# Low part of every fourth weight chunk: from a VectorE subtraction to an accumulating DMA

## The chip, the core and the metric

The kernel runs on one core of a Trainium2 chip. The metric is the device time of one execution in microseconds (us). In two timed executions the kernel before took 1624.39 and 1624.61 us, median 1624.5 us. A difference of 2% of this, about 32 us, is about what a measurement of this kernel can tell from no change.

## The reference

One encoder block over 256 tokens of width 2048 in float32. All of its large products are with weight matrices:

```python
xn = rms_norm(h, norm1_g[l])
proj = xn @ w_in[l]
z_a, q, c_kv, q_idx, k_idx, w_idx, gates = jnp.split(proj, cuts, axis=-1)
y_a = spatial_gating_unit(jax.nn.gelu(z_a), ...)
y_b = indexer_sparse_attention(q, rms_norm(c_kv, ...), q_idx, k_idx, w_idx, w_uk[l], w_uv[l])
g_a, g_b = jnp.split(jax.nn.sigmoid(gates), 2, axis=-1)
mixed = g_a * (y_a @ w_oa[l]) + g_b * (y_b @ w_ob[l])
h = h + mixed @ w_out[l]
hn = rms_norm(h, norm2_g[l])
h = h + (jax.nn.silu(hn @ w_ff_gate[l]) * (hn @ w_ff_up[l])) @ w_ff_down[l]
```

The projections, the attention's key and value matrices, the output matrices and the feed-forward network together hold some 300 MB of weights. Each weight is read once.

## The kernel before

Every product against a weight matrix is done as three passes of TensorE. An operand is split exactly into h, its upper 12 mantissa bits in the type float32r, and l, the rest; h\*h, l\*h and h\*l are added up in PSUM. The split of a weight is made on the chip, chunk by chunk, in `wchunk` (L73 to L82). A chunk is 128 partitions by 1024 float32, 512 KB, and holds two k tiles of 512 columns. Its way has four steps:

1. SP's queue issues the load of `raw` from DRAM (L80).
2. ScalarE copies `raw` to `wh` with rounding to float32r (L67): the part h.
3. VectorE subtracts, `wl = raw - wh` (L68): the part l.
4. TensorE multiplies with `wh` and `wl`.

The tiles `raw`, `wh` and `wl` come from a pool with four buffers each. So the split of chunk i+4 may be written when TensorE has done its last product with chunk i, and the load of chunk i+4 may start when VectorE has subtracted chunk i. Chunks are made in the order in which TensorE uses them, and each engine runs its instructions in the order in which they are written to its queue.

Two helpers use the chunks. `nat_group` (L89) makes blocks of 512 columns for both tiles of 128 tokens: the weights are the moving operand, 12 products of 512 columns per chunk, 6 for each of the two k tiles. For each it calls `mm3` (L84), whose second product (L86) is the first to read `wl`. `tr_group` (L104) makes transposed blocks for the index queries, the queries and the keys: the weights are the stationary operand, 24 products of 256 columns per chunk, and the third of them (L120) is the first to read `wl`.

The program goes through: the latent and the index keys (16 chunks of 592 columns), index queries and top keys, branch A's values (`v`), attention four heads at a time beside branch A's gates (`q`, `k`, `vv`, `u`), position mixing, gates and branch outputs (`g`, `oa`, `ob`), the output projection (`out`), and the feed-forward network in blocks of 512 columns (`fg` gate, `fu` up, `fd` down). A full group is 8 chunks. After a group its two PSUM banks are taken out, by ScalarE for `v`, `u`, `g` and `fg` (Gelu, Sigmoid or Silu), by VectorE for the others. There are 544 chunks of 1024 columns that go through the pool of four; 8 more, the last ones of `w_ff_down`, are split into tiles that are kept to the end.

The program is written with a scheduler that sets each engine's order from priorities and semaphores; the kernel does not write an order by hand.

Of the kernel before, what the change touches and what calls it, by code (L numbers as in the profile page):

```python
# [32 lines left out]
MARK = -3.0e38  # L33
WARM = 8  # matmuls of zeros that open the clock gate


@with_exitstack
def block_kernel(ctx: ExitStack, tc: tile.TileContext, a, out):
    """Every product against a weight matrix is float32 = three float32r passes: an operand is
    split exactly into h (its upper 12 mantissa bits, rounded) and l (the rest, 12 bits), and  # L40
    h*h + l*h + h*l is accumulated in float32."""
    nc = tc.nc
# [20 lines left out]
    def split(h, l, src, scale=None):  # L63
        """h + l = src (times a scale per partition), exactly."""
        hf = h.bitcast(F32)
        if scale is None:
            nc.scalar.activation(h, src, AF.Copy)  # L67
            nc.vector.tensor_tensor(l, src, hf, op=ALU.subtract)  # L68
        else:
            nc.scalar.activation(h, src, AF.Copy, scale=scale)  # L70
            nc.vector.scalar_tensor_tensor(l, src, scale, hf, op0=ALU.mult, op1=ALU.subtract)

    def wchunk(src, cols, keep=False):  # L73
        raw = wp.tile([P, 1024], F32, tag="raw", name="raw")
        if keep:
            h, l = (t_tile(z).rearrange("p a b -> p (a b)") for z in ("kept_h", "kept_l"))
        else:
            h = wp.tile([P, 1024], F32R, tag="wh", name="wh")
            l = wp.tile([P, 1024], F32R, tag="wl", name="wl")
        nc.sync.dma_start(raw[:, :cols], src)  # L80
        split(h[:, :cols], l[:, :cols], raw[:, :cols])
        return h, l  # L82
# [6 lines left out]
    def nat_group(w, ks, x, name):  # L89
        """[tokens, 512] blocks of x @ w for both token tiles. w: [chunks, 128, 1024] in DRAM;  # L90
        ks: its k tiles; x(k) -> the k tile's (h, l), [128, 256] each."""
        acc = [acc_tile(f"{name}_{t}") for t in range(2)]
        for c in range(len(ks) // 2):
            wh, wl = wchunk(w[c], 1024)
            for j in range(2):
                i = 2 * c + j
                xh, xl = x(ks[i])
                for t in range(2):
                    s = slice(t * P, (t + 1) * P)
                    mm3(acc[t], xh[:, s], xl[:, s], wh[:, j * 512:(j + 1) * 512],  # L100
                        wl[:, j * 512:(j + 1) * 512], i == 0, i == len(ks) - 1)
        return acc

    def tr_group(w, ks, x, name, bank=acc_tile, beside=None):  # L104
        """(x @ w).T for 512 columns of w: two banks of [128 columns, 2, 256 tokens]. beside(c) is
        called after each chunk."""
        acc = [bank(f"{name}_{b}").rearrange("p (c t) -> p c t", c=2) for b in range(2)]
        for c in range(len(ks) // 2):
            wh, wl = wchunk(w[c], 1024)
            for j in range(2):  # L110
                i = 2 * c + j
                xh, xl = x(ks[i])
                for ct in range(4):
                    s = slice(j * 512 + ct * P, j * 512 + (ct + 1) * P)
                    o = acc[ct // 2][:, ct % 2, :]
                    last = i == len(ks) - 1
                    nc.tensor.matmul(o, wh[:, s], xh, start=(i == 0 and ct % 2 == 0), stop=False,  # L117
                                     skip_group_check=True)
                    nc.tensor.matmul(o, wh[:, s], xl, start=False, stop=False, skip_group_check=True)  # L119
                    nc.tensor.matmul(o, wl[:, s], xh, start=False, stop=last, skip_group_check=True)  # L120
            if beside is not None:
                beside(c)
        return acc

    def rsqrt(dst, src, mul, add, m, name):
        """dst = 1 / sqrt(src * mul + add), [128, m]: Newton's steps from the bits' guess, each left
        with a factor (a power of two) that the last product takes out."""
        v = sp.tile([P, m], F32, tag=f"rs_v{m}", name=f"{name}_v", bufs=2)
# [14 lines left out]
    def transposed(src, name, h, l, scale=None):  # L143
        """src [128 tokens, 2, 512] -> h, l [128, 4, 256 tokens]."""
        for b in range(2):
# [11 lines left out]

# [1 line left out]
    # while the first loads run: the activation table, and the tensor engine's clock  # L159
    warm = const.tile([P, 512], BF16, name="warm")  # L160
# [31 lines left out]
    def sumsq(ss, src, n):  # L192
        """ss[:, n, t] = the sums of squares of src [128, 2, 512]'s rows."""
        for t in range(2):
            junk = sp.tile([P, 512], BF16, tag="junk", name="junk")
            nc.scalar.activation(junk, src[:, t], AF.Square, accum_out=ss[:, n, t:t + 1])
# [9 lines left out]

# [1 line left out]
    KS = list(range(KT))  # L208
# [58 lines left out]

# [1 line left out]
    index_queries(1, acc_tile)  # L269
# [22 lines left out]
    for hp in range(8):  # L292
        score_pair(hp)
    # keep: 0 where a key is kept, else a large negative; [tile 1's 256 keys | tile 0's 128]
    keep = sp.tile([P, T + P], F32, name="keep")
    for t in (1, 0):
        w = (t + 1) * P
        nc.vector.memset(score[t][0:CHUNK, w - CHUNK:w], NEG)
        for i in range(TOPK // 8):
# [4 lines left out]
                                op0=ALU.is_gt, op1=ALU.mult)  # L304
    # r1 * B_HEAD_DIM ** -0.5, for tile 1 and tile 0
    ascale = sp.tile([P, 2], F32, name="ascale")
    for t in range(2):
        nc.vector.tensor_scalar(ascale[:, 1 - t:2 - t], r1[:, t:t + 1], P ** -0.5, None, op0=ALU.mult)

# [1 line left out]
    stats = sp.tile([P, 2, 4, 6], F32, name="stats")  # L311
# [34 lines left out]

# [1 line left out]
    yb = []  # L348
# [53 lines left out]

# [1 line left out]
    ws = n_tile("ws").rearrange("p a b -> p (a b)").rearrange("p (g q) -> p g q", g=GROUPS)  # L404
# [21 lines left out]

# [1 line left out]
    def gate(g):  # L428
# [22 lines left out]

# [1 line left out]
    ss2 = sp.tile([P, 4, 2], F32, name="ss2")  # L453
# [13 lines left out]

# [1 line left out]
    at = []  # L469
# [17 lines left out]

    # the last block's weights stay split on chip, so that token tile 0 is through before tile 1
    ends = (4, 8, NFB - 1)
# [55 lines left out]
def _layout(np, i):  # L545
    """The arrays as the program reads them: only cut, transposed and joined."""
    x = np.asarray(i["x"])[0]
# [8 lines left out]
    z, q, c, qi, ki, wi, g = np.split(w_in, cuts, axis=1)  # L556
    col = lambda v: np.asarray(v).reshape(-1, P).T  # noqa: E731
    ln = np.stack([np.asarray(i["a_ln_g"])[0].reshape(4, 512), np.asarray(i["a_ln_b"])[0].reshape(4, 512)], 1)
# [40 lines left out]
```

## Time and profile before

| | |
|---|---|
| timed executions | 1624.39 and 1624.61 us |
| median | 1624.5 us |
| span of the profiled execution, first to last instruction | 1624.0 us |
| what lies around the span, against the median | 0.5 us |
| bytes moved over the span | 307.54 MB |
| engines with the most busy time | TensorE, then its weight loads, VectorE, ScalarE |

The profile is one execution with hardware records of each instruction. Its span is within 0.5 us of the timed median, so a term worked out from its rows can be set against the median as it stands. In the rows PE is TensorE's products, PEld its weight loads, DVE VectorE, ACT ScalarE, POOL GpSimd, and SPq the queue of SP that issues the loads. A row names the line, the engine, the operation, and the tiles as out<-in.

Ends of matmuls are modelled and matmuls overlap, so a row's 0.39 us is longer than the step from one matmul's start to the next. Steps are read here from the starts.

### The profile page before, as it was taken

How to read it: one execution, taken by the hardware profiler on the slowest of the kernel's cores; microseconds unless marked ns; L12 is line 12 of the kernel's file. 1: busy time of each engine (PE TensorE's matmuls, PEld its weight loads, DVE VectorE, ACT ScalarE, POOL GpSimd, SP SyncE). 2: the span in 40 equal slices, each digit the busy share in tenths (PEclk: the TensorE clock that was granted, in tenths of full speed). 3: DMA queues.
4: the chain of work that ended last, by engine and by line, in shares of the span. 5: the costliest groups of instructions: out<-in, count | busy, mean ns of one | idle time of the engine just before them, and what ended most of it. 6: DMA issues, size and time to landing. Idle time of an engine off the chain costs nothing.

```text
span 1624.0 us, 20315 instructions
## 1 busy us (share of the span) xinstructions
PE 1613.2 (99%) x7954; PEld 1358.6 (84%) x7954; DVE 893.8 (55%) x1084; ACT 742.9 (46%) x891; POOL 1.6 (0%) x8
## 2 busy tenths in 40 slices
PE   9999999999999999999999999999999999999997
PEld 8988989889788888888888888888888888888886
DVE  5695665565754444555556444455545454554575
ACT  6554464554544444444444444444344444334452
POOL 0000000000000000000000000000000000000000
PEclk9999999999999999999999999999999999999999
DMA  8646555555545555555655555555655555555671
GB/s 302 214 138 201 187 168 182 170 177 175 163 161 192 193 193 194 193 183 196 236 186 185 194 185 190 186 191 186 194 191 192 186 191 188 193 192 194 218 253 59
DMA packets 88128, 307.54 MB, mean 189 GB/s; under 512 B 10272, under 2 KB 10528, under 8 KB 88032
## 3 DMA queue, kind: packets, MB, share of 16 engines
q1 hardware_dynamic: 88032, 306.25, 57.2%
q8 instruction: 62, 1.02, 0.2%
q14 instruction: 34, 0.28, 0.0%
HBM read 304.11 MB, written 2.10 MB: 189 GB/s over the span
## 4 chain that ended last, share of the span: by engine, by line
PE 99%; DMA 0%; DVE 0%; ACT 0%; SPq 0%; issue 0%; ACTq 0%
PE fg L85 5%; PE fg L86 5%; PE fg L87 5%; PE fu L86 5%; PE fu L87 5%; PE fu L85 5%; PE fd L87 4%; PE fd L85 4%; PE fd L86 4%; PE g L86 4%; PE g L85 4%; PE g L87 4%; PE q L120 2%; PE q L119 2%; PE q L117 2%; PE u L87 2%
## 5 line engine op out<-in xcount | busy, mean ns | idle before, releaser
L68 DVE TENSOR_TENSOR wl<-raw,wh 128x1024 fp32r<-128x1024 f32 (+1 forms) x560 | 678.9, 1212 | 668.6 <-ACT wh L67 668.2
L67 ACT ACTIVATE wh<-raw 128x1024 fp32r<-128x1024 f32 (+1 forms) x560 | 587.8, 1050 | 764.9 <-PE fu L87 139.4
L86 PE MATMUL fg<-wl,hh 128*128 128x512 f32 x352 | 137.8, 392 | 0.0
L87 PE MATMUL fg<-wh,hl 128*128 128x512 f32 x352 | 137.7, 391 | 0.0
L85 PE MATMUL fg<-wh,hh 128*128 128x512 f32 x352 | 137.1, 390 | 0.0
L85 PE MATMUL fu<-wh,hh 128*128 128x512 f32 x352 | 136.9, 389 | 0.0
L86 PE MATMUL fu<-wl,hh 128*128 128x512 f32 x352 | 136.9, 389 | 0.0
L87 PE MATMUL fu<-wh,hl 128*128 128x512 f32 x352 | 136.9, 389 | 0.0
L86 PE MATMUL fd<-wl,ah 128*128 128x512 f32 x320 | 124.8, 390 | 0.0
L87 PE MATMUL fd<-wh,al 128*128 128x512 f32 x320 | 124.8, 390 | 0.0
L85 PE MATMUL fd<-wh,ah 128*128 128x512 f32 x320 | 124.6, 389 | 0.0
L87 PE MATMUL g<-wh,xl 128*128 128x512 f32 x256 | 100.9, 394 | 0.0
L85 PE MATMUL g<-wh,xh 128*128 128x512 f32 x256 | 100.7, 393 | 0.0
L86 PE MATMUL g<-wl,xh 128*128 128x512 f32 x256 | 99.9, 390 | 0.0
L85 PEld LDWEIGHTS fu<-wh,hh 128*128 128x128 f32 x352 | 66.1, 188 | 13.7
L86 PEld LDWEIGHTS fu<-wl,hh 128*128 128x128 f32 x352 | 66.1, 188 | 13.7
L87 PEld LDWEIGHTS fu<-wh,hl 128*128 128x128 f32 x352 | 66.1, 188 | 13.7
L85 PEld LDWEIGHTS fg<-wh,hh 128*128 128x128 f32 x352 | 66.1, 188 | 13.5
L86 PEld LDWEIGHTS fg<-wl,hh 128*128 128x128 f32 x352 | 66.1, 188 | 13.4
L87 PEld LDWEIGHTS fg<-wh,hl 128*128 128x128 f32 x352 | 66.2, 188 | 13.2
L120 PE MATMUL q<-xh,wl 128*128 128x256 f32 x256 | 72.4, 283 | 0.0
L119 PE MATMUL q<-xl,wh 128*128 128x256 f32 x256 | 72.4, 283 | 0.0
(220 smaller groups left out, 2722.7 us busy)
## 6 DMA issues: line engine op xcount, KB each, us to landing
raw<-in_w_fg SPq DMA_DIRECT2D x88, 512.0 KB, 3.3
raw<-in_w_fu SPq DMA_DIRECT2D x88, 512.0 KB, 3.3
raw<-in_w_fd SPq DMA_DIRECT2D x88, 512.0 KB, 3.3
raw<-in_w_z SPq DMA_DIRECT2D x64, 512.0 KB, 3.3
raw<-in_w_g SPq DMA_DIRECT2D x64, 512.0 KB, 3.3
raw<-in_w_q SPq DMA_DIRECT2D x32, 512.0 KB, 3.3
raw<-in_w_oa SPq DMA_DIRECT2D x32, 512.0 KB, 3.3
raw<-in_w_ob SPq DMA_DIRECT2D x32, 512.0 KB, 3.3
```

The source lines that it names most:

```text
L67: nc.scalar.activation(h, src, AF.Copy)
L68: nc.vector.tensor_tensor(l, src, hf, op=ALU.subtract)
L85: nc.tensor.matmul(o, lh, rh, start=start, stop=False, **kw)
L86: nc.tensor.matmul(o, lh, rl, start=False, stop=False, **kw)
L87: nc.tensor.matmul(o, ll, rh, start=False, stop=stop, **kw)
L117: nc.tensor.matmul(o, wh[:, s], xh, start=(i == 0 and ct % 2 == 0), stop=False, skip_group_check=True)
L119: nc.tensor.matmul(o, wh[:, s], xl, start=False, stop=False, skip_group_check=True)
L120: nc.tensor.matmul(o, wl[:, s], xh, start=False, stop=last, skip_group_check=True)
```

## The change

For every fourth call of `wchunk` the low part is made in another way, if the chunk has 1024 columns and isn't one of the kept ones. ScalarE writes h as before, and then a second time into `wl`, with the factor -1: `wl = -h`. Then GpSimd's queue issues a DMA that reads the chunk from DRAM once more and adds it to what stands in `wl`. VectorE has no part in it.

```diff
+    n_chunks = [0]
+
     def wchunk(src, cols, keep=False):
         raw = wp.tile([P, 1024], F32, tag="raw", name="raw")
...
         nc.sync.dma_start(raw[:, :cols], src)
-        split(h[:, :cols], l[:, :cols], raw[:, :cols])
+        n_chunks[0] += 1
+        if keep or cols < 1024 or n_chunks[0] % 4:
+            split(h[:, :cols], l[:, :cols], raw[:, :cols])
+        else:
+
+            nc.scalar.activation(h, raw, AF.Copy)
+            nc.scalar.activation(l, h.bitcast(F32), AF.Copy, scale=-1.0)
+            nc.gpsimd.dma_start(l, src, accum_op=ALU.add)
         return h, l
```

All other lines of the diff take comments away; lines move by up to 9. L67 and L68 stay, the two new ScalarE lines are L88 and L89, and the new DMA is L90; the products L85, L86 and L87 become L94, L95 and L96.

There are 136 such DMAs. Since a full group has 8 chunks, they fall on the fourth and the eighth chunk of every full group, and their `wl` is always the same one of the four buffers.

On ScalarE's queue, before, around the fourth chunk of an up group `fu`: two Silu's take the gate group's banks out, and then the split of the fourth chunk follows.

```order
559 L67 ACTIVATE wh_8332<-raw_8331 128x1024 [waits DMAHW1_49,DVE_49,PE_49]
560 L67 ACTIVATE wh_8350<-raw_8349 128x1024 [waits DMAHW2_49,DVE_49,PE_49]
561 L475 ACTIVATE s2_8308<-fg2_0_8162,r2_r_7520 128x512 [waits PE_49]
562 L475 ACTIVATE s2_8308<-fg2_1_8163,r2_r_7520 128x512 [waits PE_49]
563 L67 ACTIVATE wh_8368<-raw_8367 128x1024 [waits DMAHW3_49,DVE_49]
564 L67 ACTIVATE wh_8386<-raw_8385 128x1024 [waits DMAHW4_49,DVE_49,PE_49]
565 L67 ACTIVATE wh_8404<-raw_8403 128x1024 [waits DMAHW5_49,DVE_49,PE_49]
```

The same place on ScalarE's queue in the changed kernel, one block later (`fg3` in place of `fg2`):

```order
665 L67 ACTIVATE wh_8731<-raw_8730 128x1024 [waits DMAHW1_49,DVE_49,PE_49]
666 L67 ACTIVATE wh_8749<-raw_8748 128x1024 [waits DMAHW2_49,DVE_49,PE_49]
667 L484 ACTIVATE s3_8707<-fg3_0_8559,r2_r_7592 128x512 [waits PE_49]
668 L484 ACTIVATE s3_8707<-fg3_1_8560,r2_r_7592 128x512 [waits PE_49]
669 L88 ACTIVATE wh_8767<-raw_8766 128x1024 [waits DMAHW3_49,Activation_49]
670 L89 ACTIVATE wl_8768<-wh_8767 128x1024 [waits DMASW5_49,Activation_49]
671 L67 ACTIVATE wh_8786<-raw_8785 128x1024 [waits DMAHW4_49,DVE_49,PE_49]
672 L67 ACTIVATE wh_8804<-raw_8803 128x1024 [waits DMAHW5_49,DVE_49,PE_49]
```

The chunk's `wh` keeps its place behind the two Silu's; the `wl` of L89 stands between it and the next chunk's `wh`. Its wait is for the accumulating DMA before (DMASW5), which wrote the same buffer.

On TensorE's queue, before, the first products with that fourth chunk (`wl_8682` is its low part):

```order
5289 L87 MATMUL fu3_1_8625<-wh_8663,hl1_7147 128x512
5290 L85 MATMUL fu3_0_8624<-wh_8681,hh1_7146 128x512 [waits Activation_49]
5291 L86 MATMUL fu3_0_8624<-wl_8682,hh1_7146 128x512 [waits DVE_49]
5292 L87 MATMUL fu3_0_8624<-wh_8681,hl1_7147 128x512
5293 L85 MATMUL fu3_1_8625<-wh_8681,hh1_7146 128x512
```

The same products in the changed kernel (`wl_8768` is the low part):

```order
5289 L96 MATMUL fu3_1_8711<-wh_8749,hl1_7215 128x512
5290 L94 MATMUL fu3_0_8710<-wh_8767,hh1_7214 128x512 [waits Activation_49]
5291 L95 MATMUL fu3_0_8710<-wl_8768,hh1_7214 128x512 [waits DMASW6_49]
5292 L96 MATMUL fu3_0_8710<-wh_8767,hl1_7215 128x512
5293 L94 MATMUL fu3_1_8711<-wh_8767,hh1_7214 128x512
```

No product has moved here; the chunk's second product waits for the DMA (DMASW6) where it waited for VectorE. On SP's queue the load of the fourth chunk behind such a chunk waits for ScalarE instead of VectorE.

## Rows read from the trace of the kernel before

**Rows 1.** The page: busy us, share of the span, instructions, by engine

```profile
PE 1613.2 (99%) x7954; PEld 1358.6 (84%) x7954; DVE 893.8 (55%) x1084; ACT 742.9 (46%) x891; POOL 1.6 (0%) x8
```

**Rows 2.** The page: the chain that ended last, shares by engine

```profile
PE 99%; DMA 0%; DVE 0%; ACT 0%; SPq 0%; issue 0%; ACTq 0%
```

**Rows 3.** The waits of PE: waiter <- waited for: us, times, longest

```profile
PE warm_ps L166 <- DVE warm L161: 1.2, 1, 1.2
PE kv L85 <- ACT xh L70: 0.6, 1, 0.6
```

**Rows 4.** Groups by shape on ACT, DVE: count | busy us, mean ns | idle

```profile
L67 ACT ACTIVATE wh<-raw 128x1024 fp32r<-128x1024 f32 x544 | 576.6, 1060 | 757.4 <-PE fu L87 139.4 <-PE fg L87 121.6 <-PE fd L87 109.7
...
L68 DVE TENSOR_TENSOR wl<-raw,wh 128x1024 fp32r<-128x1024 f32 x544 | 666.5, 1225 | 659.9 <-ACT wh L67 659.5
```

**Rows 5.** Timeline inside an fu group: start us, us, engine, what [idle before <-releaser]

```profile
1001.19 0.39 PE L87 MATMUL fu<-wh,hl 128*128 128x512 f32 x1
...
1001.42 0.39 PE L85 MATMUL fu<-wh,hh 128*128 128x512 f32 x1
...
1001.62 1.06 ACT L67 ACTIVATE wh<-raw 128x1024 fp32r<-128x1024 f32 x1 [1.66 <-PE fu L87]
1001.64 0.39 PE L86 MATMUL fu<-wl,hh 128*128 128x512 f32 x1
...
1002.71 1.23 DVE L68 TENSOR_TENSOR wl<-raw,wh 128x1024 fp32r<-128x1024 f32 x1 [1.49 <-ACT wh L67]
...
1004.34 1.06 ACT L67 ACTIVATE wh<-raw 128x1024 fp32r<-128x1024 f32 x1 [1.66 <-PE fu L87]
...
1005.43 1.23 DVE L68 TENSOR_TENSOR wl<-raw,wh 128x1024 fp32r<-128x1024 f32 x1 [1.50 <-ACT wh L67]
```

**Rows 6.** Timeline of ACT where an fg group ends

```profile
1038.03 1.06 ACT L67 ACTIVATE wh<-raw 128x1024 fp32r<-128x1024 f32 x1 [1.66 <-PE fg L87]
1040.07 1.37 ACT L475 ACTIVATE s<-fg,r_r 128x512 f32<-128x512 f32 x2 [0.98 <-PE fg L87]
1041.33 1.05 ACT L67 ACTIVATE wh<-raw 128x1024 fp32r<-128x1024 f32 x1
```

**Rows 7.** Timeline of ACT inside a q group (transposed)

```profile
312.74 1.06 ACT L67 ACTIVATE wh<-raw 128x1024 fp32r<-128x1024 f32 x1 [1.77 <-PE q L119]
315.62 1.06 ACT L67 ACTIVATE wh<-raw 128x1024 fp32r<-128x1024 f32 x1 [1.82 <-PE q L119]
```

**Rows 8.** DMA of the page: queue share; issues xcount, KB, median us to landing

```profile
q1 hardware_dynamic: 88032, 306.25, 57.2%
...
raw<-in_w_fu SPq DMA_DIRECT2D x88, 512.0 KB, 3.3
...
xn<-in_x SPq DMA_DIRECT2D x4, 512.0 KB, 8.8
```

**Rows 9.** DMA busy tenths, 1001.58 to 1012.46 us, 40 slices; a load then

```profile
DMA  4199598980009589992000977988410069699840
...
raw<-in_w_fg SPq DMA_DIRECT2D x4, 512.0 KB, 4.3
```

**Rows 10.** Windows: stretch, length, busy PE PEld DVE ACT POOL, PEclk, DMA, GB/s

```profile
0.00:10.00 10.00, 8.16 (x28) 5.62 (x29) 4.34 (x9) 6.07 (x11) 1.63 (x8) 1.00 0.78 254
...
1610.00:1624.00 14.00, 5.20 (x35) 4.61 (x33) 6.98 (x20) 3.80 (x10) 0.00 (x0) 0.75 0.30 111
```

## The prediction

> **What bounds the kernel now.** I began with the busy times and the chain that ended last. PE is busy for 1613.2 of 1624.0 us [rows 1], and the chain is PE for 99% of its length [rows 2]. Then the waits of PE: 1.2 and 0.6 us in all, both in the start [rows 3]. So nothing that VectorE, ScalarE or the DMA queues do holds PE up today, and the subtraction that the change takes away is not waited for. VectorE stands idle for 659.9 us before those subtractions, until ScalarE's `wh`, and ScalarE in turn waits for PE's last product with a chunk [rows 4]. The supply runs at PE's pace and has slack. A gain could come only out of the 1.8 us of waits and the two ends of the program, which have no such chunk. The question is whether the new way of making `wl` still fits into the slack.
>
> The slack is read from the timeline of one group [rows 5]. At 1001.19 PE starts its last product with a chunk; at 1001.42 it goes on to the next. At 1001.62 ScalarE starts `wh` in the buffer that came free, and the next `wh` starts at 1004.34: a chunk takes PE 2.72 us. The product at 1001.64 is the first that reads `wl` in the chunk begun at 1001.42. The chunk now being split is the one three later, so its `wl` is read first at 1001.64 + 3 x 2.72 = 1009.80, or 8.18 us after `wh` starts. Today `wl` is ready at 1002.71 + 1.23 = 1003.94. That leaves 5.9 us unused.
>
> **The change, part by part.** It removes 136 VectorE subtractions of 1.225 us, 167 us, beside waits [rows 4]: worth nothing by itself. It adds 136 copies on ScalarE; by the row for the same shape 1.060 us each, 144 us [rows 4], which lifts ScalarE from 742.9 to 887 us, 55% of the span. Four chunks take ScalarE 5 x 1.06 = 5.3 of 10.88 us, so this is hidden as well. The next chunk's `wh` does not begin until 2.72 us after this one's, and the two copies take 2.12. Where a bank's take-out stands before them, the next `wh` is late by some tenths, within its 5.9 us of slack.
>
> What isn't hidden by anything else is the chain behind the copies. `wh` ends at 1.06, `-h` at 2.12; the hand-over to the next engine costs 0.03 (1002.68 to 1002.71 in [rows 5]). The accumulating DMA can be issued 2.15 us after `wh` starts and must have landed at 8.18. **Its margin is 6.03 us** from issue to landing. Two kinds of chunk have another margin:
>
> - Behind a group that ScalarE takes out. The regular `wh` would start at 1038.03 + 2.72 = 1040.75; it starts at 1041.33, behind two Silu's [rows 6]. Margin 6.03 - 0.58 = 5.45 us. By the order of ScalarE's queue that is the fourth chunk behind 4 `v`, 4 `u`, 8 `g` and 11 `fg` groups: 27 chunks.
> - In transposed groups a chunk takes PE 315.62 - 312.74 = 2.88 us [rows 7], 0.16 longer, three times: margin 6.5 us. These are 8 chunks of queries and 4 of index queries, 12 in all.
>
> The other 97 are taken as ordinary. If a DMA lands later than its margin, PE stands still at the chunk's second product, and everything behind it on PE's queue with it; so do the next `wh`s, which wait for PE. GpSimd's queue has nothing else but the next such DMA, 10.88 us later. A stall cannot be won back: the chain for the next chunk in this buffer begins when PE has left this one. So each microsecond over the margin counts in full, 136 times.
>
> **How long does the DMA take?** No row of this trace shows an accumulating DMA or one issued by GpSimd, so it is bounded from both sides. From below: the plain load of the same 512 KB lands 3.3 us after issue [rows 8]; at that price it is hidden, and the change costs nothing. From above: 8.8 us, the longest median landing of 512 KB in this program, beside the crowded loads of the start [rows 8]. That would be 97 x 2.77 + 27 x 3.35 + 12 x 2.3 = 387 us. Less than nothing is excluded at both ends, because PE doesn't wait today.
>
> Between them I build it up. Loads hold the 16 engines for 57.2% of 1624.0 us [rows 8], 929 us for 306.25 MB, or 1.59 us per 512 KB. Adding needs a second operand: what stands in `wl` must be read as well as the chunk. If reads set the pace, that is another 1.6 us: 3.3 + 1.6 = 4.9 us. And it isn't alone. In four chunk times the engines show four bursts of some 2 us with gaps of about 0.7 us between them [rows 9], and in that stretch a plain load already lands after 4.3 us in place of 3.3. With 3.2 us of data, a transfer that begins to move some 4 us after `wh` starts is still moving when the load for the following chunk comes (that one is issued behind the next subtraction, at 1005.43 + 1.23 = 1006.66, or 5.0 us [rows 5]). Sharing with it costs up to that load's own 1.6 us: 6.5 us. I take the 6.5, the end with a full collision, because the issue by software on GpSimd is not in the sum and can only add to it. It is also close to two plain landings one behind the other, 6.6 us.
>
> With 6.5: 97 ordinary chunks x 0.47 = 46 us, 27 chunks behind a take-out x 1.05 = 28 us, 12 transposed ones x 0 = 0. Sum 74 us on the profiled span of 1624.0 us, 1698 us; against the median, 0.5 us above the span, 1698.5 us. I say 1699.
>
> The Trainium skill bears on both terms. In "Collectives: The Full Stack", section "The bandwidth ceiling: the fold count and why AG ≠ RS ≠ AR", it says that an add inside the DMA path costs no time of its own, but that its two source reads share one ring and so halve the rate. That agrees with the 1.6 us; a reader who holds the add to be free altogether would have 4.9 us and no stall. No row here shows it. The page "DMA: Bandwidth & Descriptors", section "Specifications", gives about 1 us to the first byte for a DMA that GpSimd issues against 0.6 for one from SP. By it the landing would be 0.4 us later, an estimate of 128 us in place of 74, or 1752 us. No row here shows that either, and it stays out of the sum.
>
> Bytes as a bound: 136 more transfers bring the engines from 57.2% to 57.2 + 136 x 3.2 / 1624 = 84%. That is below full, so loads are stretched but not short: a load issued 5 us into its period has some 8 us until it is needed.
>
> **Rivals.** First, hidden (not slower): the add streams at the rate of a copy, or falls into the gaps of [rows 9], and lands within some 5.4 us. Then PE waits nowhere and the time is 1624.5, whatever the engines' shares say. For it: 3.3 us for the plain load, 4.9 with a second read, both under every margin. Against it: 4.3 us for a plain load in a busy stretch. It decides at a landing of 6.15 us, where the loss is 97 x 0.12 + 27 x 0.70 = 31 us, 2%. Second, far slower: the accumulating path has a rate of its own well under a copy's, or GpSimd needs microseconds to issue. At 8 us to landing it is 97 x 1.97 + 27 x 2.55 + 12 x 1.5 = 278 us, 1902. For it: nothing measured here; against it: the engines move 512 KB in under 2 us even in bursts. Third, the change is a little faster: VectorE with 167 us less work lets some take-out come sooner. Against it stand the 1.8 us of waits [rows 3].
>
> That PE's clock falls in the stalls is not to be expected: it stayed at 1.00 with PE busy for 8.16 of 10 us and fell to 0.75 with 5.20 of 14 [rows 10]; here PE would be busy some 10.9 of 11.5 us.
>
> **How the numbers follow.** Landing between 6.15 and 7.3 us, the forecast: 0.40, with 1656 to 1807 us for its own range (at 7.3: 97 x 1.27 + 27 x 1.85 + 12 x 0.8 = 183). Hidden or nearly so: 0.38. Far slower: 0.20. Faster by over 2%: 0.02, since PE's busy time alone is 99% of the span. Slower by over 2% is then 0.60. The range takes in the hidden case whole and the slow case up to a landing of about 7.7 us (97 x 1.67 + 27 x 2.25 + 12 x 1.2 = 237): 1622 to 1862 us.
>
> **What would show it.** Right: PE's waits list L95 behind the accumulating DMA into `wl`, some 120 times with about half a microsecond, more for the chunks behind a take-out; the landing of the 136 DMAs stands near 6.5 us; DVE is busy near 727 us and ACT near 887; the engines' share is near 80%. Wrong: no PE wait on a DMA (hidden), a landing beyond 8 us, or stalls at `wh` rather than `wl`, which would mean late loads, a step that I cost at nothing.

## The result and the profile after

The changed kernel took 1773.99 and 1790.41 us, median 1782.2 us, against 1624.5 us before: a ratio of 1.097 with an interval of 1.085 to 1.109. That is 157.7 us more; the forecast was 74.5 us more. The profiled execution has a span of 1788.6 us, 164.6 us above the 1624.0 of before, and its rows are read against that.

Page of the changed kernel: busy us by engine; the shares of the DMA queues (q1 carries SP's loads, q0 GpSimd's DMAs; packets, MB, share of 16 engines); the chain that ended last. Then, of another view, the span and the mean granted clock of TensorE.

```profile
PE 1661.8 (93%) x7954; PEld 1370.7 (77%) x7954; DVE 735.2 (41%) x948; ACT 882.7 (49%) x1027; POOL 119.4 (7%) x144
...
q1 hardware_dynamic: 88032, 306.25, 51.2%
q0 software_dynamic: 19584, 71.31, 24.1%
...
PE 54%; DMA 32%; ACT 10%; issue 3%; DVE 0%; ACTq 0%; SPq 0%; POOLq 0%
```

```profile
core 0: 1788.6 us, clock 0.982
```

Beside [rows 1] and [rows 2]: VectorE lost its 136 subtractions (893.8 to 735.2 us) and ScalarE gained its 136 copies (742.9 to 882.7). The chain, 99% PE before, now runs through DMAs for a third of its length. PE is idle for 126.8 us in place of 10.8, and busy for 48.6 us more with the same 7954 products. Part of the longer busy time is the lower clock, 0.982 in place of 0.998; how much is worked out below.

The waits of PE in the changed kernel (waiter <- waited for: us in all, times, longest); [rows 3] had two rows of 1.2 and 0.6 us.

```profile
PE fu L95 <- DMA wl<-in_w_fu: 19.9, 13, 3.4
PE fd L95 <- DMA wl<-in_w_fd: 18.3, 10, 5.0
PE fg L95 <- DMA wl<-in_w_fg: 13.9, 12, 3.3
PE q L129 <- DMA wl<-in_w_q: 11.9, 4, 3.8
PE g L95 <- DMA wl<-in_w_g: 10.8, 9, 2.3
```

With the six rows below these (9.9 to 2.5 us each) PE waits 112.9 us in 73 waits for the accumulating DMA, 1.55 us on the mean. It waits where the prediction put it, at the first product that reads `wl`. There is no row with a wait for `wh`, so no load was late.

Landing of the 136 accumulating DMAs, by the tile's view; and from the page, the plain load beside them (3.3 us before, [rows 8]).

```profile
DMA to landing us min/median/max: 5.2/6.3/9.8
```

```profile
raw<-in_w_fg SPq DMA_DIRECT2D x88, 512.0 KB, 4.4
```

Timeline of the changed kernel (start us, us, engine, what [idle before <-releaser]): two such chunks, the first of them begun at 999.41 behind a take-out.

```profile
999.41 1.06 ACT L88 ACTIVATE wh<-raw 128x1024 fp32r<-128x1024 f32 x1
1001.32 1.06 ACT L67 ACTIVATE wh<-raw 128x1024 fp32r<-128x1024 f32 x1 [0.85 <-PE fu L96]
1002.29 1.04 ACT L89 ACTIVATE wl<-wh 128x1024 fp32r<-128x1024 f32 x1
```

```profile
1003.62 0.86 POOL L90 DMA_DIRECT2D wl<-in_w_fu  x1 [12.54 <-ACT wl L89]
...
1010.55 0.50 PE L95 MATMUL fu<-wl,hh 128*128 128x512 f32 x1 [3.38 <-DMA wl<-in_w_fu]
...
1013.22 1.06 ACT L88 ACTIVATE wh<-raw 128x1024 fp32r<-128x1024 f32 x1 [5.40 <-PE fu L96]
...
1014.31 1.06 ACT L89 ACTIVATE wl<-wh 128x1024 fp32r<-128x1024 f32 x1
...
1015.66 0.86 POOL L90 DMA_DIRECT2D wl<-in_w_fu  x1 [11.17 <-ACT wl L89]
```

Two things here are not in the prediction. In the first chunk `-h` does not follow `wh`: the next chunk's `wh` stands between them on ScalarE's queue, and the copy ends at 1003.33 in place of 1001.53 (999.41 + 2.12). So PE waits 3.38 us. This is the order that the scheduler chose; in 19 of the 136 chunks other work stands between the two copies. And the hand-over from ScalarE to GpSimd takes 1015.66 - 1015.37 = 0.29 us; the prediction priced it at 0.03.

The clock, in windows of the changed kernel (stretch, length, busy PE PEld DVE ACT POOL, PEclk, DMA share, GB/s):

```profile
1230.70:1237.50 6.80, 4.96 (x23) 3.78 (x22) 3.46 (x3) 2.12 (x2) 0.00 (x0) 1.00 0.95 236
1237.54:1240.95 3.41, 3.41 (x10) 2.63 (x9) 0.69 (x1) 0.00 (x0) 0.00 (x0) 0.50 0.59 193
1240.95:1247.80 6.85, 6.85 (x31) 5.66 (x31) 1.92 (x2) 4.25 (x4) 0.86 (x1) 1.00 0.58 135
```

PE stood for 1.84 of 6.80 us, in one wait of 1.8 us for `wl`; then the granted clock is 0.50 (1.2 GHz) for 3.41 us, though PE is busy throughout, and back at 1.00 (2.4 GHz). At half speed, 3.41 us of work cost an estimated 1.7 us more. There are 15 stretches at 0.50 in this execution. The same view, asked for all 15, sums their length and each engine's busy time:

```profile
sum 62.99, PE 52.59 PEld 44.56 DVE 5.15 ACT 4.71 POOL 0.00; mean PE 3.51 PEld 2.97 DVE 0.34 ACT 0.31 POOL 0.00
```

PE is busy for 52.59 us at half speed, so the clock costs some 26 us, an estimate. In the kernel before there was one stretch at 0.50, at the end, with PE idle.

So the 164.6 us are: 113 of waits for `wl`, some 26 of lower clock, some 8 of a longer first product behind each of the 73 waits (0.50 us in place of 0.39), and some 18 that the views don't take apart, most of it in PE's busy time.

### The profile page after: what moved, and what is told of

Its sections match the earlier page's. It is cut to its first block, busy times and chain, and to the rows that moved or that the text cites. A ratio compares the mean times of both kernels' runs of the same rounds, so it can differ in the third digit from the quotient of the medians.

```text
span 1788.6 us, 20583 instructions
## 1 busy us (share of the span) xinstructions
PE 1661.8 (93%) x7954; PEld 1370.7 (77%) x7954; DVE 735.2 (41%) x948; ACT 882.7 (49%) x1027; POOL 119.4 (7%) x144
## 3 DMA queue, kind: packets, MB, share of 16 engines
q1 hardware_dynamic: 88032, 306.25, 51.2%
q0 software_dynamic: 19584, 71.31, 24.1%
## 4 chain that ended last, share of the span: by engine, by line
PE 54%; DMA 32%; ACT 10%; issue 3%; DVE 0%; ACTq 0%; SPq 0%; POOLq 0%
DMA wl<-in_w_fu 6%; DMA wl<-in_w_fg 5%; ACT wl L89 4%; ACT wh L88 4%; DMA wl<-in_w_fd 4%; DMA wl<-in_w_g 4%; PE fd L95 3%; PE fg L95 3%; PE fd L96 3%; DMA wl<-in_w_z 3%; PE fg L96 3%; PE fd L94 2%; PE fu L95 2%; PE fg L94 2%; PE fu L96 2%
## 5 line engine op out<-in xcount | busy, mean ns | idle before, releaser
L68 DVE TENSOR_TENSOR wl<-raw,wh 128x1024 fp32r<-128x1024 f32 (+1 forms) x424 | 512.1, 1208 | 885.3 <-ACT wh L67 884.9
L67 ACT ACTIVATE wh<-raw 128x1024 fp32r<-128x1024 f32 (+1 forms) x424 | 443.3, 1046 | 467.2 <-PE fg L96 82.1
L88 ACT ACTIVATE wh<-raw 128x1024 fp32r<-128x1024 f32 x136 | 144.0, 1059 | 295.0 <-PE fu L96 66.0
L95 PE MATMUL fu<-wl,hh 128*128 128x512 f32 x352 | 140.3, 399 | 20.2 <-DMA wl<-in_w_fu 19.9
L95 PE MATMUL fg<-wl,hh 128*128 128x512 f32 x352 | 140.9, 400 | 14.0 <-DMA wl<-in_w_fg 13.9
L89 ACT ACTIVATE wl<-wh 128x1024 fp32r<-128x1024 f32 x136 | 144.1, 1060 | 3.7
L95 PE MATMUL fd<-wl,ah 128*128 128x512 f32 x320 | 127.7, 399 | 18.3 <-DMA wl<-in_w_fd 18.3
L96 PE MATMUL fg<-wh,hl 128*128 128x512 f32 x352 | 139.1, 395 | 0.0
L94 PE MATMUL fg<-wh,hh 128*128 128x512 f32 x352 | 138.4, 393 | 0.0
L96 PE MATMUL fu<-wh,hl 128*128 128x512 f32 x352 | 138.3, 393 | 0.0
L94 PE MATMUL fu<-wh,hh 128*128 128x512 f32 x352 | 138.3, 393 | 0.0
L96 PE MATMUL fd<-wh,al 128*128 128x512 f32 x320 | 126.2, 394 | 0.0
L94 PE MATMUL fd<-wh,ah 128*128 128x512 f32 x320 | 126.0, 394 | 0.0
L95 PE MATMUL g<-wl,xh 128*128 128x512 f32 x256 | 101.5, 396 | 10.8 <-DMA wl<-in_w_g 10.8
L94 PE MATMUL g<-wh,xh 128*128 128x512 f32 x256 | 101.5, 397 | 0.0
L96 PE MATMUL g<-wh,xl 128*128 128x512 f32 x256 | 100.4, 392 | 0.0
L95 PEld LDWEIGHTS fu<-wl,hh 128*128 128x128 f32 x352 | 66.8, 190 | 40.8 <-DMA wl<-in_w_fu 27.1
L95 PEld LDWEIGHTS fg<-wl,hh 128*128 128x128 f32 x352 | 66.9, 190 | 33.3 <-DMA wl<-in_w_fg 20.1
L95 PEld LDWEIGHTS fd<-wl,ah 128*128 128x128 f32 x320 | 60.9, 190 | 35.4 <-DMA wl<-in_w_fd 22.9
L94 PEld LDWEIGHTS fu<-wh,hh 128*128 128x128 f32 x352 | 66.8, 190 | 14.3
L94 PEld LDWEIGHTS fg<-wh,hh 128*128 128x128 f32 x352 | 66.8, 190 | 14.0
```

Source lines behind the costliest of these rows:

```text
L88: nc.scalar.activation(h, raw, AF.Copy)
L89: nc.scalar.activation(l, h.bitcast(F32), AF.Copy, scale=-1.0)
L94: nc.tensor.matmul(o, lh, rh, start=start, stop=False, **kw)
L95: nc.tensor.matmul(o, lh, rl, start=False, stop=False, **kw)
L96: nc.tensor.matmul(o, ll, rh, start=False, stop=stop, **kw)
```

## The experiments

Each ratio is against the kernel before, timed beside the runs. Where nothing is said, diffs are against the changed kernel.

**Is it the wait, or the traffic and ScalarE's work?** Two kernels, run with a third on the adding.

*e2_aside10*: VectorE subtracts for every chunk as before; `-h` and the accumulating DMA go into a tile of their own that no product reads (another pool has one buffer fewer for it).

```diff
-            nc.scalar.activation(l, h.bitcast(F32), AF.Copy, scale=-1.0)
-            nc.gpsimd.dma_start(l, src, accum_op=ALU.add)
+            split(h, l, raw)
+            z = wp.tile([P, 1024], F32R, tag="wz", name="wz", bufs=1)
+            nc.scalar.activation(z, h.bitcast(F32), AF.Copy, scale=-1.0)
+            nc.gpsimd.dma_start(z, src, accum_op=ALU.add)
```

> VectorE's subtraction for wl is back for every chunk. The copy -h and the accumulating DMA are made as well, but into a tile of their own that TensorE doesn't read (4 KB per partition, taken from the pool of [128, 2, 512] tiles, 10 in place of 11). All the traffic and ScalarE work of the change, no wait of TensorE for it. Theory A (the landing of wl): 1625 to 1640 us, PE busy near 1615, clock 0.99 or more. Rival C (the engines are too full, loads come late, or ScalarE's 144 us more are in the way): above 1680 us, with PE waiting for wh.

Measured: 1631.62 us, ratio 1.004 (1.002 to 1.006), as theory A has it. The longest wait of PE, and the landing of the DMAs, which is longer than in the changed kernel:

```profile
PE fd L95 <- ACT wh L67: 2.7, 1, 2.7
```

```profile
DMA to landing us min/median/max: 5.1/7.8/9.0
```

All the DMA traffic and all of ScalarE's copies together cost 7 us where PE waits for none of it. The loss is the wait, with what follows from it.

*e4_bufs5np9*: a fifth buffer for `wh` and `wl` (`bufs=5`; another pool has two buffers fewer for it), which gives the chain one chunk time more.

> The change with five buffers for wh and wl in place of four (room from the pool of [128, 2, 512] tiles, 9 in place of 11; raw stays at four): 2.72 us more margin for every chunk. Theory A: about 10 us of stalls left, clock 0.99 or more, 1630 to 1650 us. Rival C: the bytes are the same, so above 1720 us.

Measured: 1641.47 us, ratio 1.010 (1.007 to 1.013). Landing is as long as ever, 5.1/6.7/11.8 us, and PE waits 11.3 us in all. So 141 of the 158 us go with a larger margin, while the bytes stay.

*e1_plain*: the DMA copies the chunk over `-h` and does not add, so the products with `wl` are not those of the low part.

```diff
-            nc.gpsimd.dma_start(l, src, accum_op=ALU.add)
+            nc.gpsimd.dma_start(l, src)
```

> Leaves out the adding: the same DMA from GpSimd's queue, behind the same copies and at the same places, copies the chunk over -h (wl then holds the whole weight, not its low part). Theory A (the second read): each packet takes 0.33 us in place of the loads' 0.16 and the transfer 3.4 to 5.7 us; without the add it takes about half, lands some 4 us after the issue and inside nearly every margin; only the chunks whose -h stands behind other work on ScalarE still stall. 1630 to 1645 us. Rival B (the issue by GpSimd is what costs: 0.3 us to hand over, 1.57 us to the first packet): the landing stays near 6 us and the time above 1720 us.

Measured: 1654.34 us, ratio 1.017 (1.013 to 1.021). From the page and the tile's view of this kernel:

```profile
q0 software_dynamic: 19584, 71.31, 14.0%
```

```profile
DMA to landing us min/median/max: 3.3/4.7/7.1
```

The 71.31 MB took the engines 14.0% of 1649.9 = 231 us; with the adding it was 24.1% of 1788.6 = 431 us, 1.87 times as long. So the adding costs 1.6 us of the median landing, as the prediction priced it for a second read, and with it go 128 of the 158 us (the time stays 9 us above the expected range). That it is the reading and not the addition itself, no run shows apart.

**Making the margin larger.**

*e3_lfirst*: ScalarE writes `-h` first, straight from `raw`, and `wh` after it.

```diff
+            nc.scalar.activation(l, raw, AF.Copy, scale=-1.0)
             nc.scalar.activation(h, raw, AF.Copy)
-            nc.scalar.activation(l, h.bitcast(F32), AF.Copy, scale=-1.0)
```

> ScalarE writes wl = -h first, straight from raw with the factor -1 (the rounding is symmetric), and wh after it. The DMA can be issued 1.09 us earlier. Theory A: each stall shrinks by up to 1.09 us; of the 114 us of PE's waits for the DMA some 45 are left, and the clock's dips shrink with them: 1670 to 1690 us. Rival D (the collision with the next load sets the end, whenever the transfer begins): the transfers last longer, and the time stays above 1740 us.

Measured: 1685.49 us, ratio 1.036 (1.022 to 1.051), in theory A's range. The DMA goes out one copy earlier, but `raw` comes free one copy later, and landing grew to 6.6 us.

*e5_wllast*: for such a chunk TensorE does the products that read `wl` last, as the ninth to the twelfth.

```diff
+            late = n_chunks[0] % 4 == 0
+            for part in (0, 1) if late else (2,):
...
+                        elif part == 0:
+                            nc.tensor.matmul(acc[t], xh[:, s], wh[:, wj], start=i == 0, stop=False)
+                            nc.tensor.matmul(acc[t], xl[:, s], wh[:, wj], start=False, stop=False)
+                        else:
+                            nc.tensor.matmul(acc[t], xh[:, s], wl[:, wj], start=False, stop=last)
```

> The change, but in each such chunk TensorE does the eight products with wh first and the four with wl after them (16 and 8 in transposed groups): the first product that reads wl is the ninth and not the second, 7 x 0.227 = 1.59 us later. Theory A: 1.59 us more margin, some 30 us of PE's waits left of 114, 1650 to 1675 us. Rival D (the transfer stretches with the loads whatever its start): above 1740 us.

Measured: 1652.4 us, ratio 1.017 (1.011 to 1.023), and PE waits 12.6 us for the DMA. A margin 1.59 us larger takes away 130 us, somewhat more than expected: most of the stalls lie within 1.6 us of the margin.

*e6_both*: the two together.

> Both remedies: wl = -h written first and straight from raw (1.09 us), and the products with wl last (1.59 us). Margin up by 2.68 us, about that of the fifth buffer. Theory A: 10 to 15 us of stalls left, 1630 to 1650 us, not under the kernel before, which has no wait to lose. A rival of A's that all of the time comes from PE's lowered clock, once begun, would leave the clock below 0.99.

A miss: 1681.86 us, ratio 1.035 (1.032 to 1.038), no better than the first alone. From the tile's view and the timeline of ScalarE:

```profile
DMA to landing us min/median/max: 6.5/7.8/10.0
```

```profile
999.88 1.06 ACT L89 ACTIVATE wh<-raw 128x1024 fp32r<-128x1024 f32 x1 [0.80 <-PE fu L117]
1001.81 1.06 ACT L88 ACTIVATE wl<-raw 128x1024 fp32r<-128x1024 f32 x1 [0.87 <-PE fu L119]
```

Since `wl` is now read last, its buffer comes free last: L88 (now the one that writes `-h`) waits for PE's last product, L119, and runs behind `wh`. The order in which a buffer is read decides when it can be written again, so the two gains don't add.

**The late copies.** *e8_nolate*: the 19 chunks whose `-h` the scheduler put behind other work of ScalarE are subtracted by VectorE; 117 DMAs are left.

```diff
-        if keep or cols < 1024 or n_chunks[0] % 4:
+        add = not (keep or cols < 1024 or n_chunks[0] % 4)
+        if add:
+            n_add[0] += 1
+        if not add or n_add[0] - 1 in late:
```

> The change, but the 19 chunks whose -h stood behind other ScalarE work (attention, output projection, index queries and a few more) are subtracted by VectorE as before; 117 DMAs are left. Theory A with placement: these 19 made some 29 of the 114 us of stalls; 85 us are left, and with the clock's part 1735 to 1755 us. Rival G (placement does nothing, the stalls of the 19 belong to collisions like the others): about 117/136 of the loss, 1750 to 1775 us, with the stalls spread as before.

Measured: 1737.15 us, ratio 1.069 (1.066 to 1.072): 45 us less for a seventh of the DMAs, in the range of theory A and under that of G. PE's waits for the DMA fall from 112.9 to 75.6 us, and the clock is 0.992 in place of 0.982. In the trace of the changed kernel, 29 us of PE's stalls stand behind these 19 chunks (the idle time of PE at each one's landing, added up).

**The clock.** *e9_pool3*: no second read; GpSimd does the subtraction three times over, so that PE stalls for a computation.

```diff
-            nc.scalar.activation(l, h.bitcast(F32), AF.Copy, scale=-1.0)
-            nc.gpsimd.dma_start(l, src, accum_op=ALU.add)
+            for _ in range(3):
+                nc.gpsimd.tensor_tensor(l, raw, h.bitcast(F32), op=ALU.subtract)
```

> No accumulating DMA and no -h: GpSimd subtracts wl = raw - wh for each such chunk, three times over the same tile, so that wl comes late by compute alone. It asks whether stalls lower PE's clock without any more DMA traffic. If one subtraction takes 2.5 us, wl is ready 9 us after wh starts, a stall near 1 us, and raw is held longer: 1720 to 1900 us. Theory H (the clock follows PE's stalls): mean granted clock 0.99 or less once stalls pass some 100 us. Rival I (it follows the DMA's load): the clock stays at 0.995 or more.

Measured: 2036.37 us, ratio 1.253 (1.249 to 1.258), 136 us above the expected range. Page and clock of this kernel, and the largest row of PE's waits:

```profile
PE 1738.6 (86%) x7954; PEld 1419.9 (70%) x7954; DVE 1173.9 (58%) x948; ACT 744.9 (37%) x891; POOL 1153.1 (57%) x416
...
q1 hardware_dynamic: 88032, 306.25, 41.9%
...
L90 POOL TENSOR_TENSOR wl<-raw,wh 128x1024 fp32r<-128x1024 f32 x408 | 1151.5, 2822 | 836.9 <-ACT wh L88 797.4
```

```profile
core 0: 2031.6 us, clock 0.947
```

```profile
PE fu L95 <- POOL wl L90: 47.0, 22, 3.9
```

With the rows below it PE waits 241 us for GpSimd's subtractions, and 38 us for VectorE.

With DMA engines 41.9% busy in place of 75.3%, the clock is lower still, as theory H says and against I: it falls without the added traffic, where PE stalls. GpSimd's work is new here too, so this kernel alone doesn't prove that the stalls do it; the window above, with its stall ahead of the fall, points the same way.

**What makes a transfer long?** The prediction named the load for the following chunk. Three kernels ask that.

*e7_oneq*: the loads go through GpSimd's queue as well, in one row with the accumulating DMAs (`nc.gpsimd.dma_start(raw[:, :cols], src)`).

> The change with the plain loads of raw issued from GpSimd's queue too, so that the accumulating DMA and the load that follows it are in one queue, in this order. Theory E (collision: 59 of the 136 transfers take over 4.2 us because the load of the following chunk shares the engines, and these make 83 of 114 us of stalls): a transfer that is first in its queue no longer shares with that load, most take 3.2 to 3.6 us, stalls fall to 20 to 45 us, 1650 to 1690 us. Rival F (transfers are long for another reason, as the chip's memory or the adding itself): still 4.5 to 5.5 us for some 60 of them, above 1740 us. The loads' own issue by GpSimd could also be late, which would show as PE waiting for wh.

A miss: 1792.94 us, ratio 1.103 (1.095 to 1.112), landing 5.1/6.3/8.6. The timeline of GpSimd shows why one queue doesn't help:

```profile
1008.57 0.53 POOL L82 DMA_DIRECT2D raw<-in_w_fg  x1 [2.85 <-ACT wh L88]
1009.67 0.88 POOL L90 DMA_DIRECT2D wl<-in_w_fu  x1 [0.57 <-ACT wl L89]
```

The load that `wh`'s end releases is issued 1.1 us ahead of the transfer, as it is from SP's queue. The loads of the start came late here, as the expectation allowed: 12.0 us of the time are one wait for `wh` in the latent's chunks.

*e10_hold*: the load that the following chunk's subtraction releases is held until the accumulating DMA has landed. GpSimd reads one column of the following chunk's `raw` and of the `wl` in question, and the next load into that `raw` waits for the reading.

```diff
+        if added:
+            mark = sp.tile([P, 1], F32, tag="mark", name="mark", bufs=2)
+            nc.gpsimd.tensor_tensor(mark, raw[:, :1], added.pop().bitcast(F32)[:, :1], op=ALU.add)
...
             nc.gpsimd.dma_start(l, src, accum_op=ALU.add)
+            added.append(l)
```

> The change, but the load that follows an accumulating DMA on SP's queue (the fifth chunk on) is held until the DMA has landed: GpSimd adds one column of the next chunk's raw and one of the new wl into a spare tile, so that this raw comes free only then. No transfer shares the engines with that load. Theory E (collision): nearly all transfers land 5.2 to 5.6 us after the issue, the ordinary chunks stop stalling, some 29 us are left at the 19 chunks whose -h is late, the clock is at 0.99 or more: 1650 to 1680 us. Rival F (transfers are long for another reason): landing still 6.3 us in the median, above 1740 us; held loads that come late would show as PE waiting for wh.

A miss: 1793.65 us, ratio 1.104 (1.099 to 1.108), and landing 5.2/6.4/9.0 us as before. The hold worked, as SP's waits show:

```profile
SPq L83 <- POOL mark L87: 566.6, 134, 7.3
```

So long transfers don't need that load. (What the held load does instead is told below.) *e11_holdnolate*, the same without the 19 late chunks, missed in the same way:

> Both: the following load is held, and the 19 chunks with a late -h are subtracted by VectorE (117 DMAs). If collision and placement together are the loss, nothing of note is left: 1626 to 1645 us, clock at 0.995 or more. If a third cause is at work, above 1660 us.

1779.77 us, ratio 1.095 (1.092 to 1.098), landing 5.2/6.5/9.0 us.

That leaves the loads ahead of the transfer. Two chunks of the changed kernel, by the timeline of SP's queue and of GpSimd, and then the landing of each one's DMA, by the DMA view of the stretch (KB, us from issue to landing):

```profile
653.52 0.33 SPq L82 DMA_DIRECT2D raw<-in_w_oa  x1
656.19 0.33 SPq L82 DMA_DIRECT2D raw<-in_w_oa  x1
657.55 0.86 POOL L90 DMA_DIRECT2D wl<-in_w_oa  x1 [11.17 <-ACT wl L89]
...
1023.67 0.33 SPq L82 DMA_DIRECT2D raw<-in_w_fg  x1
1025.18 0.33 SPq L82 DMA_DIRECT2D raw<-in_w_fg  x1
1026.54 0.86 POOL L90 DMA_DIRECT2D wl<-in_w_fg  x1 [10.01 <-ACT wl L89]
```

```profile
wl<-in_w_oa POOLq DMA_DIRECT2D x1, 512.0 KB, 5.3
...
wl<-in_w_fg POOLq DMA_DIRECT2D x1, 512.0 KB, 7.3
```

In both a load goes out 1.36 us before the DMA, when `wh` has been written and `raw` is free. In the first the load before that one is 2.67 us ahead of it, in the second only 1.51. Two loads hold the engines for 2 x 1.59 us. In the packet records the first packet of such a DMA comes 1.6 us after its issue. In the second chunk some of the 16 engines still have packets of the loads then. Those engines begin the transfer late, and it ends with a few engines working alone: 0.5 us before the last packet ends, transfers of over 3.8 us have 3 packets under way on the mean, shorter ones 14. Counted over the 136 transfers of the changed kernel, first packet to last takes 3.5 us (median) where no load is left in the engines at its start, and 5 us where loads still fill 0.2 us or more of its first 0.6. Of the 56 of the first kind, 7 take over 3.8 us; of the 56 with 0.1 us or more of loads, 49 do. By the timeline of SP's queue, 47 DMAs have two loads less than 2 us apart ahead of them, and 42 of these take over 3.8 us; of the other 89, 26 do. Chunks whose -h is prompt and whose transfer takes over 3.8 us, 64 of them, carry 84 us of stalls; the other 53 prompt ones carry 2 (PE's idle time at each landing, which with the 29 of the late ones makes 115 us, against 113 in the view of the waits).

Two kernels test it. *e12_raw5* is the control: a fifth `raw` buffer, with one buffer fewer in another pool. *e13_raw5hold* puts the hold on the chunk's own `raw`, whose load it delays with all that stand behind it on SP's queue.

```diff
-        raw = wp.tile([P, 1024], F32, tag="raw", name="raw")
+        raw = wp.tile([P, 1024], F32, tag="raw", name="raw", bufs=5)
...
             nc.gpsimd.dma_start(l, src, accum_op=ALU.add)
+            mark = sp.tile([P, 1], F32, tag="mark", name="mark", bufs=2)
+            nc.gpsimd.tensor_tensor(mark, raw[:, :1], l.bitcast(F32)[:, :1], op=ALU.add)
```

> Control for the next two: a fifth raw buffer and nothing else (the pool np has 10 buffers for it in place of 11). Loads are issued at the same moments, when a raw becomes free, only for a chunk that is used one later. Both theories: the transfers collide as before, landing 6.3 us, 1765 to 1795 us.

> The fifth raw buffer, and the load that follows when the chunk's own raw becomes free, and with it the loads behind it on SP's queue, held until the accumulating DMA has landed (GpSimd reads raw and wl once behind it). Theory L: a transfer is long because the load issued at the end of the chunk's wh, and the one 1.5 us before it, still have packets in the engines when its first packets come; some engines begin late and finish late. Then landing falls to 5.2 to 5.5 us, the stalls of the 117 chunks whose -h is prompt nearly vanish, those of the 19 late ones (29 us) stay: 1650 to 1685 us. Theory F: the spread belongs to the accumulating transfer itself. Then landing stays at 6.3 us and the time near 1780 us.

The control took 1769.56 us, ratio 1.089 (1.084 to 1.094), landing 5.0/5.8/9.7. With the hold it is 1713.39 us, ratio 1.055 (1.051 to 1.059):

```profile
DMA to landing us min/median/max: 5.0/5.2/9.9
```

```profile
PE fu L97 <- DMA wl<-in_w_fu: 9.4, 5, 4.1
PE q L131 <- DMA wl<-in_w_q: 8.3, 3, 3.6
PE fd L97 <- DMA wl<-in_w_fd: 6.9, 2, 4.0
```

Landing fell as theory L said, and PE's waits for the DMA from 112.9 us (90.2 in the control) to 49.3. The transfers that begin among a load's packets (0.1 us or more in the first 0.6) fell from 56 of 136 (42 in the control) to 13. In e10_hold they had risen to 110, since the held loads came out just ahead of the next transfer, and 80 of the 110 took over 3.8 us. So e10_hold traded one load for another, and e13_raw5hold holds back every load from the end of `wh` to the landing; neither run by itself tells the load ahead from the load behind. The packet records do: in e10_hold 86 transfers take over 3.8 us though from 1.5 us after their first packet on less than one of 16 engines is at work on a load, and in the changed kernel less than one of 16 is between 1.25 and 2.75 us after it, in long and short transfers alike (means). The time stays 28 us above the range of theory L. *e14_raw5holdnolate* takes the 19 late chunks away as well:

> The same without the 19 late chunks, which VectorE subtracts. Theory L: nothing is left over the margin, 1628 to 1650 us. Theory F: as without the hold, near 1737 us.

1671.79 us, ratio 1.029 (1.027 to 1.031), again above the range, by 22 us, but far under the other theory's 1737. What is left are 27.6 us of waits, nearly all for DMAs that were still long: 21 of 117, 4.4 us from first to last packet in the median. Sixteen of the 21 again begin among a load's packets; why the others are long was not tried.

No version is faster than the kernel before. The nearest, e2_aside10 and e4_bufs5np9, are 0.4 and 1.0% slower; with PE busy for 99% of the span before, there was nothing to win.

## Why the prediction was right and wrong

**Right.** The sign, and why: nothing waited for the subtraction, and the new chain's landing lay over its margin. The waits stand at L95. VectorE's 735 us (forecast 727), ScalarE's 883 (887) and the engines' share of 51.2 + 24.1 = 75% (80%) came out as worked. The adding takes the engines 1.87 times as long as a copy, near the twice that the prediction priced. The Trainium skill says in "Collectives: The Full Stack", section "The bandwidth ceiling: the fold count and why AG ≠ RS ≠ AR", that two source reads halve the rate. The 1.87 of these runs is near that factor.

The Trainium skill gives in "DMA: Bandwidth & Descriptors", section "Specifications", about 1 us to the first byte for a DMA that GpSimd issues and about 0.6 for one from SP. The packet records show a difference of this kind: where no packet was under way, a load's first packet came 1.23 us after its issue from GpSimd's queue (e7_oneq, 32 loads) and 0.95 us from SP's (the changed kernel, 39 loads). An accumulating DMA's came after 1.6 us. The sum left this out; a transfer that met no load landed in 5.2 us at the least, where the sum without collision had 4.9.

**Wrong in size: the term "97 ordinary chunks x 0.47 + 27 x 1.05 = 74 us".** It took one landing, 6.5 us, for every DMA. The median was that: 6.3, and 0.26 more of hand-over. But there are two kinds of transfer, with median landings of 5.4 us (68 that take up to 3.8 us from first to last packet) and 7.1 us (the other 68), and a stall counts one side only: 73 waits of 1.55 us, 113 us, where 124 short ones were forecast. For the 117 prompt chunks alone it is 86 us, 0.74 per chunk where the sum has 0.54 (74 / 136). Three more things were missing from the sum:

- "`wh` ends at 1.06, `-h` at 2.12", for every chunk: it doesn't for 19 of them. They make 29 us of stalls, and 45 us of the time went with them in e8_nolate.
- "That PE's clock falls in the stalls is not to be expected": it fell, for some 26 us. [Rows 10] gave two stretches at the ends of the program, and the forecast set a mean of 10.9 of 11.5 us against them. The stalls were longer than that mean, and after one of 1.8 us the granted clock was 0.50 for 3.41 us.
- The longer first product behind each wait, some 8 us, and some 18 us not taken apart.

**Wrong in cause: "that transfer is still moving when the load for the following chunk comes".** In the changed kernel that load hardly moves while the transfer does, by the packets above, and transfers stayed long where it was held (e10_hold). The loads ahead do it for most of the long ones, and the change itself put them there. `raw` of such a chunk comes free at the end of `wh`, not of a subtraction 1.23 us later, so the two loads ahead of the DMA can follow each other after 1.51 us in place of 2.72; in 47 of the 136 chunks they are less than 2 us apart. The change's section says that the load waits for ScalarE now; the prediction did not price this moved DMA. Left at about its old time it would be no better: in e3_lfirst it is released one copy later, runs beside the transfer, and landing is 6.6 us. That the median came out near 6.5 us was luck: the collision that gave the number was the wrong one, and few transfers land near it.

**Rivals.** Hidden fell: it would have held with a landing of 5.2 us for all (the smaller margin, 5.45, less 0.26 of hand-over), which no kernel here reached. Far slower, by a rate of its own or a slow issue, fell: the adding takes 1.87 times a copy's time, and the issue row is 0.86 us.

## What to carry to other kernels

Price a hidden chain by the spread of its slowest link, not by its median: here 52 of the 136 DMAs landed later than 6.8 us, half a microsecond over the median, and what the early ones spare doesn't pay for the late ones. When an edit changes who reads a buffer last, look for the load that it releases and ask what that load now runs into. And for a chain that is too long, try one buffer more first (141 of 158 us here): shortening the chain moved other waits in (e3_lfirst, e6_both). Reading the late operand last gained nearly as much (130 us, e5_wllast).

## What the runs showed of the hardware

- A stall of 1.8 us of a TensorE that is otherwise full can cost nearly as much again in clock: 3.41 us at 0.50 after it. It does not always: the changed kernel has 73 waits for `wl` and 15 stretches at 0.50. In e9_pool3 the mean fell to 0.947.
- Subtractions on GpSimd slow VectorE: with 408 of them (2.82 us each) VectorE's busy time for the same 948 instructions rose from 735.2 to 1173.9 us. In that kernel a VectorE subtraction that ran wholly beside one of GpSimd's took 2.24 us in the median (135 of them), one that ran beside none 1.21 (94). The expectation did not have this; it is a part of why that kernel was slower than its range, with 38 us of PE's waits for VectorE beside 241 for GpSimd.
- A 512 KB accumulating DMA from GpSimd landed in 5.0 to 5.2 us at the least (6.5 in e6_both), a copy of the same bytes in 3.3 us (e1_plain).
